# One decoder layer on one core: ten operand splits handed from VectorE to GpSimd, and the attention masks written earlier in a visit

## The chip, the core and the metric

The kernel runs on one core of a Trainium2 chip. Five engines work beside each other: TensorE (PE in the profile, its weight loads PEld), VectorE (DVE), ScalarE (ACT), GpSimd (POOL) and SyncE (SP), which here only issues transfers. Each engine works through its own list of instructions in order; what stands on which list, and where, is settled when the program is built. The metric is the device time of one execution in microseconds (us), the median over several runs.

## The reference

One layer: a normalised input times one wide matrix gives the inputs of a state-space branch and of an attention branch. Both end in a projection, are gated and added, and go through `w_out`, a second norm and the residual. What matters here is the attention with its forgetting term, and the projection of the state-space branch.

```
for blk in range(seqlen // 128):
    q0, q1 = blk * 128, (blk + 1) * 128
    s = einsum('bhqd,bhkd->bhqk', q[:, :, q0:q1], k[:, :, :q1]) * scale
    s = s + fcum[:, :, q0:q1, None] - fcum[:, :, None, :q1]
    s = where(kpos <= qpos, s, -inf)
    outs.append(einsum('bhqk,bhkd->bhqd', softmax(s), v[:, :, :q1]))
...
p_ssm = einsum('ble,ed->bld', y_ssm, w_branch_ssm)
p_att = einsum('ble,ed->bld', y_att, w_branch_att)
merged = sigmoid(g_ssm) * p_ssm + sigmoid(g_att) * p_att
```

The sequence has 1024 positions, the model 1024 columns, and there are 16 heads of 64.

## The kernel before, in words

**Products.** Every wide product is done for a pair of 128 output columns with seven block products in place of eight (`Pair`, `Stream`), so the 1024 x 1024 moving matrix is turned into seven operands: `b11`, `b21`, `-b22` and the differences `t1`, `-t2`, `t3`, `t4`. In this order they lie in the tiles x0 to x6. Each operand has four slabs of 128 x 512 (index j), so one matrix makes 28 blocks. Each block is kept as a high part in a reduced format (x0h and so on) and a low part, the remainder (x0l): three matmuls with high and low parts replace one. `Operands.split` (line 265) makes them: ScalarE copies the raw block into the high part (line 278, or 275 with a sign), and VectorE subtracts it from the raw block, which leaves the low part (line 279, or 276). Column weights are split in the same way (lines 350 and 351, `wop`).

**Replacing operands.** There is one set of operand tiles. When the last product that reads an operand of one matrix is done, its tile is loaded with the next matrix's block and split. `ops_s` (line 1166) holds the operands of the state-space branch's output, which replace those of the layer's input late in the attention. `ops_a` and `ops_w` follow later.

**Attention.** Eight pairs of heads are worked through in six visits each (the loop at line 1697, m = 0 to 47; hp is the pair, g the visit in it). A visit computes scores for two query blocks against one half of the keys (`scores`, line 1491): TensorE writes `s`, VectorE adds the forgetting rows `fb` and finds the minimum (line 1512; a block in which a mask is needed reads a masked copy in the free end of `ex` in place of `fb`), ScalarE takes the exponential (line 1516). TensorE turns the result (`turned`, tile pt), ScalarE and, for one block in four, VectorE copy it to `p` (lines 1555 and 1553), and the next visit multiplies it with the values (`weighted`, tile av). Turning and scores share four PSUM buffers, so scores of a visit need the copies of the visit before. Between these steps the visit places half products of the stream (`stream.halves`), which fill TensorE's time.

**Masks.** `mask` (line 1374) adds a triangle to 128 columns of `fb` in place, `masked` (line 1383) writes a masked copy into `ex`; both are pairs of GpSimd instructions. In the kernel before they are called at the end of `loads(m)` (line 1625), behind the visit's first half products and their chores.

**Order.** Instructions given to `pin` keep the order in which the program is written; the others are placed by the scheduler that builds the lists. All masks, splits and most stores on GpSimd's list are pinned, so whatever waits there holds up all that stands behind it. Without a pin are the four stores of the gates `ga` that go out by GpSimd (`tanh_gate`, line 645).

Of the kernel before, what the change touches and what calls it, by code (L numbers as in the profile page):

```python
# [12 lines left out]
ALU = mybir.AluOpType  # L13
# [6 lines left out]
NK = D // P  # L20
# [66 lines left out]
def hybrid_layer(ctx: ExitStack, tc, a, out):  # L87

    nc = tc.nc
# [31 lines left out]
    ys_dram = tc.dram_tile([NK, P, T], F32, name="ys_dram")  # L121
# [11 lines left out]
    def pin(op):  # L133
        return tc.keep_in_program_order(op)
# [24 lines left out]
    class Operands:  # L159
# [6 lines left out]
        BLOCKS = {"b11": (0, 0), "b12": (0, 1), "b21": (1, 0), "b22": (1, 1)}  # L166
        LESS = {"t1": ("b12", "b11"), "t2": ("b22", "t1"), "t3": ("t2", "b11"), "t4": ("t2", "b21")}

        def __init__(self, name, src, there=lambda k, h: True, order=lambda op: op, queue=nc.gpsimd):
            self.src, self.there, self.order, self.queue = src, there, order, queue  # L170
            self.copy = src
            self.tiles, self.left, self.made, self.at, self.step = {}, {}, set(), {}, 0
            self.lows, self.most, self.lag = {}, 1, {}
            self.dram = {n: tc.dram_tile([KH, P, HALF], F32, name=f"{n}_{name}") for n in self.LESS}
# [90 lines left out]
        def split(self, name, j, raw=None):  # L265
            h, l = (t[:, j, :] for t in self.tiles[name])
            if name.strip("-") in self.lows:

                pin(nc.scalar.activation(h, h.bitcast(F32), AF.Copy, scale=-1.0 if name[0] == "-" else 1.0))
                self.left[name].remove(j)  # L270
                return
            if raw is None:
                raw = l.bitcast(F32)
            if name[0] == "-":
                pin(nc.scalar.activation(h, raw, AF.Copy, scale=-1.0))
                pin(nc.vector.scalar_tensor_tensor(l, raw, -1.0, h, ALU.mult, ALU.subtract))
            else:
                pin(nc.scalar.activation(h, raw, AF.Copy))
                pin(nc.vector.tensor_tensor(l, raw, h, ALU.subtract))
            self.left[name].remove(j)  # L280

        def direct(self, j, y, x):
# [192 lines left out]
    class Stream:  # L475
# [74 lines left out]
        def half(self):  # L550
            if self.run is None:
                if self.at == len(self.steps):
                    return False
                p, which = self.steps[self.at]
                if which == 7 and p.ops is ops_a and "merged" not in fin:
                    return False
                if p.ops is ops_a and not all(p.ops.ready(OPERAND[which].strip("-"), j) for j in range(KH)):
                    return False
                self.ahead(False)
                for ops in self.building:  # L560
                    ops.some(OPERAND[which])
                if self.at + 1 < len(self.steps):
                    after, then = self.steps[self.at + 1]
                    after.begin(then, after.sums + (after is p and which in (5, 7)), True)
                self.run = p.do(which)
                next(self.run)
            else:
                for _ in self.run:
                    pass
                self.run = None  # L570
                p, which = self.steps[self.at]
                if p in self.following:
                    ops = self.following[p]
                    if ops not in self.building:
                        self.building.append(ops)
                    ops.open(OPERAND[which])
                self.ahead(True)
                self.at += 1
            for ops in self.building:
                if self.held is None:  # L580
                    ops.some()
                else:
                    self.held.append(ops)
            for chores in (self.chores, self.line):
                if chores:
                    chore = chores.pop(0)
                    if chore:
                        chore()
            self.count += 1
            for w in self.waiting:  # L590
                w[0] -= 1
            for w in [w for w in self.waiting if w[0] <= 0]:
                self.waiting.remove(w)
                w[1]()
            return True
# [39 lines left out]
    def tanh_gate(dram, i, queue=nc.scalar):  # L635

        t = {}

        def dst(ch):
            t[ch] = small()  # L640
            return t[ch]

        def post(ch):
            nc.scalar.activation(t[ch], t[ch], AF.Tanh, scale=0.5)
            queue.dma_start(dram[i, :, half(ch)], t[ch])

        return dst, post

# [514 lines left out]
        return dst, post, begin  # L1163

    attended = set()
    ops_s = Operands("s", lambda k, h: ys_dram[k, :, half(h)])
    ops_a = Operands("a", lambda k, h: ya_dram[k, :, half(h)], lambda k, h: (k, h) in attended)
    ops_w = Operands("w", lambda k, h: a["wo"][k * P : (k + 1) * P, half(h)], order=pin, queue=nc.sync)
    ops_a.most = 2
# [167 lines left out]
    with tc.tile_pool(name="att", bufs=1, reuse_waits="tile", side="right") as ap, tc.tile_pool(  # L1337
# [36 lines left out]
        def mask(hp, i):  # L1374

            f = fb[hp, i // 4][:, :, i % 4 * P : i % 4 * P + P]
            for e in range(2):
                pin(nc.gpsimd.tensor_tensor(f[:, e], f[:, e], far[:, P:], ALU.add))
# [246 lines left out]
        def loads(m):  # L1625

            hp, g = divmod(m, 6)
            more = hp + 1 < NK
            if g == 0:
                if hp:  # L1630
                    load_v(hp, 0)
                if not m:

                    for j in range(KH):
                        stream.line += ops_s.differences(j, difference_tile, small)
            if g == 1:
                load_q(hp, (3, 0))
            if g == 2 and more:
                load_k(hp + 1, 1)
            if g == 3:  # L1640
                load_q(hp, (2, 1))
                if more:
                    load_v(hp + 1, 1)
                if hp >= KH:
                    state["t"] = difference_tile()
                    nc.sync.dma_start(state["t"], ops_a.block("t1", hp - KH))
            if g == 4 and more:
                load_q(hp + 1, (7, 4))
            if g == (5 if more else 4) and hp >= KH:
                state["y"] = fetched("b11", hp - KH)  # L1650
            if g in (1, 3, 4):
                mask(hp, {1: 6, 3: 3, 4: 2}[g])
            if g == 4 and more:
                mask(hp + 1, 7)
            if g == 4:
                masked(hp, 1)
            if g == 5 and more:
                masked(hp + 1, 4)
            if g == 5 and more:
                load_k(hp + 1, 0)  # L1660
                load_q(hp + 1, (6, 5))

        def end(m):

# [32 lines left out]
        for m in range(6 * NK + 1):  # L1697

            if m < 6 * NK:
                hp, g = divmod(m, 6)  # L1700
                if not g:
                    heads[hp] = Heads(hp)
                for u in range(2):
                    scores(hp, g, u)
            for one in made:
                weighted(*one)
            for hd, which in end(m - 1):
                hd.free(which)
            if m == 6 * NK:
                stream.release()  # L1710
                heads[NK - 1].out(2)
                break
            for hd, which in end(m - 2):
                if hd.last and which and m < 6 * NK - 1:
                    hd.out(which)
            for fn in deferred:
                fn()
            deferred.clear()
            stream.release()
            for hd, which in end(m):  # L1720
                hd.settle(which)
            ahead, behind = room(m)
            stream.halves(ahead)

            for hd, which in end(m):
                hd.scale(which)
                hd.load_gates(which)
            if m == 6 * NK - 1:
                heads[hp].out(1)
                for fn in deferred:  # L1730
                    fn()
                deferred.clear()
            loads(m)
            made = turned(hp, g, list(end(m - 1)))
            if g in (1, 3):
                masked(hp, {1: 5, 3: 0}[g])
            for hd, which in end(m - 2):
                if not hd.last or not which:
                    hd.out(which)
            if m == 6 * NK - 1:  # L1740
                tp = pp.tile([P, HALF], F32, tag="s", bufs=4, name="tp")
                heads[hp].turn(2, tp)
                heads[hp].send(2, tp)
            stream.hold()
            stream.halves(behind)
            for hd, which in end(m if m == 6 * NK - 1 else m - 1):
                hd.take(which)
# [59 lines left out]
```

## Time and profile before

| | |
|---|---|
| three runs | 1264.94, 1266.55, 1267.89 us; median 1266.55 |
| profiled execution | 1264.74 us, its span 1263.0 us, granted TensorE clock 0.999 |
| busy share of the span | PE 98%, PEld 78%, DVE 81%, ACT 63%, POOL 27% |
| attention | from about 656 to 1105 us; the blocks of `ops_s` are split between 904 and 967 us |

Times in the views are counted in us from the start of the span. A row of the timeline gives start, length, engine, line and operation, the tiles (out<-in), shape and count, and in brackets the idle time ahead of it with the instruction that ended it. DVE instructions that follow each other overlap a little: one of 128 x 512 takes 0.69 us and the next starts 0.60 us after it. PE counts as busy until the modelled end of a matmul, so a short wait is partly hidden in the row ahead of it; the length of a run of like matmuls shows it.

### The profile page before, as it was taken

How to read it: one execution, taken by the hardware profiler on the slowest of the kernel's cores; microseconds unless marked ns; L12 is line 12 of the kernel's file. 1: busy time of each engine (PE TensorE's matmuls, PEld its weight loads, DVE VectorE, ACT ScalarE, POOL GpSimd, SP SyncE). 2: the span in 40 equal slices, each digit the busy share in tenths (PEclk: the TensorE clock that was granted, in tenths of full speed). 3: DMA queues.
4: the chain of work that ended last, by engine and by line, in shares of the span. 5: the costliest groups of instructions: out<-in, count | busy, mean ns of one | idle time of the engine just before them, and what ended most of it. 6: DMA issues, size and time to landing. Idle time of an engine off the chain costs nothing.

```text
span 1263.0 us, 20876 instructions
## 1 busy us (share of the span) xinstructions
PE 1234.3 (98%) x6864; PEld 985.6 (78%) x6864; DVE 1018.9 (81%) x1989; ACT 789.7 (63%) x1735; POOL 337.0 (27%) x384
## 2 busy tenths in 40 slices
PE   5999999999999999999999999999999999999997
PEld 3688888888888888888887777777776777688886
DVE  7998886888789878998666677776899778797975
ACT  7745765556655765567555666666786666743753
POOL 4000440014300241015111333433122232357062
PEclk9999999999999999999999999999999999999999
DMA  8243442645446542854465576666787557756932
GB/s 298 70 125 85 146 151 98 199 150 184 129 128 203 171 140 91 241 154 131 133 210 193 182 250 207 215 203 211 259 301 255 197 195 252 254 196 206 366 118 99
DMA packets 162476, 233.57 MB, mean 185 GB/s; under 512 B 15200, under 2 KB 73024, under 8 KB 162368
## 3 DMA queue, kind: packets, MB, share of 16 engines
q1 hardware_dynamic: 140160, 196.08, 48.6%
q10 hardware_dynamic: 16704, 18.06, 4.0%
q0 software_dynamic: 5504, 18.09, 3.7%
q8 instruction: 54, 0.88, 0.3%
q14 instruction: 54, 0.44, 0.1%
HBM read 162.99 MB, written 72.34 MB: 186 GB/s over the span
## 4 chain that ended last, share of the span: by engine, by line
PE 80%; DMA 7%; DVE 7%; ACT 3%; issue 2%; SPq 1%; POOL 0%; DVEq 0%; ACTq 0%; POOLq 0%
PE pb L128 34%; PE pc L128 20%; PE pd L128 7%; PE av L128 5%; PE pt L131 4%; PE s L128 4%; PE yps L128 2%; DVE wop L351 1%; PE st L128 1%; DMA xt<-in_x 1%; DVE ex L1512 1%; DMA raw<-in_wu 1%; PE tr L131 1%; PE tr_v L131 1%; DVE sum L356 1%
## 5 line engine op out<-in xcount | busy, mean ns | idle before, releaser
L350 ACT ACTIVATE wop<-sum 128x512 fp32r<-128x512 f32 x180 | 112.2, 626 | 106.3 <-DVE sum L356 49.6
L351 DVE TENSOR_TENSOR wop<-sum,wop 128x512 fp32r<-128x512 f32 x180 | 138.7, 772 | 47.6 <-ACT wop L350 45.8
L1516 ACT ACTIVATE ex<-ex,nm 128x512 f32<-128x512 f32 (+1 forms) x192 | 116.3, 607 | 75.6 <-DVE nm L1512 74.1
L410 ACT ACTIVATE s<-pb 128x512 f32<-128x512 f32 x143 | 84.6, 592 | 93.5 <-PE pb L128 91.4
L128 PE MATMUL pb<-x0h,wop 128*128 128x512 f32 x384 | 132.3, 400 | 0.0
L128 PE MATMUL pc<-x2h,wop 128*128 128x512 f32 x384 | 130.2, 397 | 0.0
L128 PE MATMUL pc<-x3h,wop 128*128 128x512 f32 x384 | 129.8, 396 | 0.4 <-DVE ot L427 0.4
L128 PE MATMUL pb<-x4h,wop 128*128 128x512 f32 x384 | 129.1, 395 | 0.0
L128 PE MATMUL pb<-x6h,wop 128*128 128x512 f32 x376 | 126.7, 395 | 1.3 <-ACT s L410 1.3
L128 PE MATMUL pb<-x5h,wop 128*128 128x512 f32 x376 | 126.8, 395 | 0.2 <-ACT s L410 0.2
L351 DVE TENSOR_TENSOR wop<-raw,wop 128x512 fp32r<-128x512 f32 x144 | 107.6, 748 | 18.5 <-ACT wop L350 18.5
L350 ACT ACTIVATE wop<-raw 128x512 fp32r<-128x512 f32 x144 | 89.7, 624 | 19.8 <-PE pd L128 10.5
L1512 DVE CUSTOM_DVE_ANT_0 ex<-s,fb 128x512 f32<-128x512 f32 (+1 forms) x128 | 78.6, 653 | 22.6 <-PE s L128 22.5
L128 PE MATMUL pd<-x1h,wop 128*128 128x512 f32 x288 | 95.8, 392 | 0.0
L211 POOL TENSOR_TENSOR wd<-wd 128x256 f32<-128x256 f32 x32 | 32.3, 1011 | 203.1 <-DMA wd<-in_wo 124.3
L128 PEld LDWEIGHTS pc<-x3h,wop 128*128 128x128 f32 x384 | 72.1, 188 | 17.7 <-issue 2.4
L128 PEld LDWEIGHTS pc<-x2h,wop 128*128 128x128 f32 x384 | 72.1, 188 | 17.5 <-issue 2.0
L128 PEld LDWEIGHTS pb<-x4h,wop 128*128 128x128 f32 x384 | 72.1, 188 | 17.2 <-issue 2.5
L128 PEld LDWEIGHTS pb<-x0h,wop 128*128 128x128 f32 x384 | 72.7, 189 | 16.1 <-issue 1.5
L128 PEld LDWEIGHTS pb<-x6h,wop 128*128 128x128 f32 x376 | 70.6, 188 | 17.7 <-ACT s L410 1.7
L128 PEld LDWEIGHTS pb<-x5h,wop 128*128 128x128 f32 x376 | 70.6, 188 | 16.7 <-issue 1.5
L131 PE MATMUL pt<-ident,ex 128*128 128x128 f32 x576 | 76.2, 274 | 2.7 <-ACT ex L1516 1.2
(311 smaller groups left out, 3025.5 us busy)
## 6 DMA issues: line engine op xcount, KB each, us to landing
raw<-in_wu SPq DMA_DIRECT2D x128, 256.0 KB
csb<-cs_dram SPq DMA_DIRECT2D x32, 256.0 KB
q<-q_dram SPq DMA_DIRECT2D x32, 256.0 KB
k<-k_dram SPq DMA_DIRECT2D x16, 512.0 KB
fb<-f_dram SPq DMA_DIRECT2D x16, 512.0 KB
rb<-st_dram SPq DMA_DIRECT2D x48, 128.0 KB
wd<-in_wo SPq DMA_DIRECT2D x40, 128.0 KB
xt<-in_x SPq DMA_DIRECT2D x8, 512.0 KB
```

Source lines behind the costliest of these rows:

```text
L128: return tc.keep_in_program_order(nc.tensor.matmul(*args, **kw))
L131: return tc.keep_in_program_order(nc.tensor.transpose(out_, in_, idn))
L211: pin(nc.gpsimd.tensor_tensor(t[out_], t[a_], t[b_], ALU.subtract))
L350: nc.scalar.activation(op[:, 0], src, AF.Copy)
L351: nc.vector.tensor_tensor(op[:, 1], src, op[:, 0], ALU.subtract)
L356: self.adds.tensor_tensor(t, x, y, ALU.add)
L410: nc.scalar.activation(s, ps, AF.Copy)
L1512: nc.vector.tensor_tensor_reduce(o, s[e][:, 0:w], f[:, e], 1.0, 3.0e38, ALU.add, ALU.min, nm)
L1516: pin(nc.scalar.activation(o, o, AF.Exp, scale=-1.0, bias=nm, accum_out=hd.at(hd.sm, i, h, e)))
```

## The change

Three edits. `Operands` gets an engine `less`, and `ops_s` is made with GpSimd: of the five operands without a sign (x0, x1, x3, x5, x6) the blocks with odd j, ten of 28, have their low part subtracted by GpSimd. The masks move from `loads` into a function of their own, called right behind the visit's scores and `settle`, ahead of its first half products; at g = 4 the copy for the next visit now comes ahead of the mask for the next pair. The four `ga` stores on GpSimd's list are pinned.

```
-        def __init__(self, name, src, there=lambda k, h: True, order=lambda op: op, queue=nc.gpsimd):
+        def __init__(self, name, src, there=lambda k, h: True, order=lambda op: op, queue=nc.gpsimd, less=nc.vector):
...
                 pin(nc.scalar.activation(h, raw, AF.Copy))
-                pin(nc.vector.tensor_tensor(l, raw, h, ALU.subtract))
+                pin((self.less if j % 2 else nc.vector).tensor_tensor(l, raw, h, ALU.subtract))
...
-            queue.dma_start(dram[i, :, half(ch)], t[ch])
+            order = pin if queue is nc.gpsimd else lambda op: op
+            order(queue.dma_start(dram[i, :, half(ch)], t[ch]))
...
-    ops_s = Operands("s", lambda k, h: ys_dram[k, :, half(h)])
+    ops_s = Operands("s", lambda k, h: ys_dram[k, :, half(h)], less=nc.gpsimd)
...
-            if g in (1, 3, 4):
-                mask(hp, {1: 6, 3: 3, 4: 2}[g])
-            if g == 4 and more:
-                mask(hp + 1, 7)
-            if g == 4:
-                masked(hp, 1)
-            if g == 5 and more:
-                masked(hp + 1, 4)
...
+        def masks(m):
+            hp, g = divmod(m, 6)
+            more = hp + 1 < NK
+            if g in (1, 3, 4):
+                mask(hp, {1: 6, 3: 3, 4: 2}[g])
+            if g == 4:
+                masked(hp, 1)
+                if more:
+                    mask(hp + 1, 7)
+            if g == 5 and more:
+                masked(hp + 1, 4)
...
                 hd.settle(which)
+            masks(m)
             ahead, behind = room(m)
             stream.halves(ahead)
```

TensorE's list stays as it is. On GpSimd's list, before, this stands at the visits g = 4 and 5 of the fifth pair of heads (about 919 to 943 us in the trace). A row with fb is `mask`, one with ex is `masked`.

```order
L1378 TENSOR_TENSOR fb<-fb,far 128x128 x2
L1387 TENSOR_TENSOR ex<-fb,far 128x128 x2
L645 DMA ga_dram<-th 128x512
L1378 TENSOR_TENSOR fb<-fb,far 128x128 x4
L1387 TENSOR_TENSOR ex<-fb,far 128x256 x2
L645 DMA ga_dram<-th 128x512
L1387 TENSOR_TENSOR ex<-fb,far 128x128 x2
```

The same place now (lines 1378, 1387 and 645 have become 1379, 1388 and 646).

```order
L1388 TENSOR_TENSOR ex<-fb,far 128x128 x2
L279 TENSOR_TENSOR x1l<-x1l,x1h 128x512
L1379 TENSOR_TENSOR fb<-fb,far 128x128 x2
L1388 TENSOR_TENSOR ex<-fb,far 128x256 x2
L1379 TENSOR_TENSOR fb<-fb,far 128x128 x2
L646 DMA ga_dram<-th 128x512
L279 TENSOR_TENSOR x1l<-x1l,x1h 128x512
L279 TENSOR_TENSOR x5l<-x5l,x5h 128x512
L1388 TENSOR_TENSOR ex<-fb,far 128x128 x2
L279 TENSOR_TENSOR x5l<-x5l,x5h 128x512
```

The copy of 256 columns was behind a store and four mask instructions; it is now behind one subtraction and two. Three subtractions stand ahead of the next copy of 128 columns, or between it and the stores.

On VectorE's list, before, the second visit of these (g = 5, about 933 to 939 us) reads as follows. Line 1512 is the scores' pass; 128x384 is the first query block, 128x256 the masked one.

```order
L1512 ISA ex,nm<-s,fb 128x384
L1512 ISA nm 128x1
L351 TENSOR_TENSOR wop<-raw,wop 128x512
L279 TENSOR_TENSOR x5l<-x5l,x5h 128x512 x2
L1512 ISA ex,nm<-s,ex 128x256
L1512 ISA nm 128x1
L1512 ISA ex,nm<-s,ex 128x256
L1512 ISA nm 128x1
L1427 RECIPROCAL sm<-sm 128x8
```

The same place now (1512 has become 1513, 1427 has become 1428).

```order
L1513 ISA ex,nm<-s,fb 128x384
L1513 ISA nm 128x1
L1513 ISA ex,nm<-s,ex 128x256
L1513 ISA nm 128x1
L351 TENSOR_TENSOR wop<-raw,wop 128x512
L1513 ISA ex,nm<-s,ex 128x256
L1513 ISA nm 128x1
L279 TENSOR_TENSOR x5l<-x5l,x5h 128x512
L1428 RECIPROCAL sm<-sm 128x8
```

The first masked pass now follows the unmasked ones at once, the second stands behind one weight split, and the x5 subtraction stands behind both.

Two visits later (about 948 to 956 us) VectorE's list before has five subtractions between the copy of a turned block and the end of the visit's four passes (the fifth, of x6, stands behind the last pass).

```order
L1553 COPY p<-pt 128x2x128
L279 TENSOR_TENSOR x3l<-x3l,x3h 128x512
L356 TENSOR_TENSOR sum<-raw 128x512
L279 TENSOR_TENSOR x3l<-x3l,x3h 128x512
L279 TENSOR_TENSOR x6l<-x6l,x6h 128x512
L1512 ISA ex,nm<-s,fb 128x512
L1512 ISA nm 128x1
L351 TENSOR_TENSOR wop<-raw,wop 128x512
L279 TENSOR_TENSOR x6l<-x6l,x6h 128x512
L1512 ISA ex,nm<-s,fb 128x512
```

Now (1553 has become 1554) there is one, and none ahead of the first pass.

```order
L1554 COPY p<-pt 128x2x128
L356 TENSOR_TENSOR sum<-raw 128x512
L1513 ISA ex,nm<-s,fb 128x512
L1513 ISA nm 128x1
L351 TENSOR_TENSOR wop<-raw,wop 128x512
L279 TENSOR_TENSOR x6l<-x6l,x6h 128x512
L1513 ISA ex,nm<-s,fb 128x512
```

Of the other four, one x3 subtraction stands earlier in VectorE's list, and the x3 and the two x6 ones with odd j are GpSimd's. SyncE's list differs in five single transfers that change places with a neighbour, ScalarE's in some ten rows at the visit around 941 us. Near the end of the attention (about 1101 us) one x3 subtraction of `ops_a` now stands behind the second masked pass in place of ahead of it.

More of the change, by code (lines that the diff above doesn't have):

```diff
@@ L167, in hybrid_layer @@
         LESS = {"t1": ("b12", "b11"), "t2": ("b22", "t1"), "t3": ("t2", "b11"), "t4": ("t2", "b21")}
-        def __init__(self, name, src, there=lambda k, h: True, order=lambda op: op, queue=nc.gpsimd):
-            self.src, self.there, self.order, self.queue = src, there, order, queue
+        def __init__(self, name, src, there=lambda k, h: True, order=lambda op: op, queue=nc.gpsimd, less=nc.vector):
+            self.src, self.there, self.order, self.queue, self.less = src, there, order, queue, less
             self.copy = src
```

## The prediction

> **What bounds the kernel now.** I read the page's busy times first, then the busy time by stretches, then what TensorE waited for, then the timeline of the stretch that stood out, engine by engine. The page:
>
> ```profile
> PE 1234.3 (98%) x6864; PEld 985.6 (78%) x6864; DVE 1018.9 (81%) x1989; ACT 789.7 (63%) x1735; POOL 337.0 (27%) x384
> ```
>
> TensorE is the bound over the span, so an edit that leaves its list alone can gain only what TensorE waits. Busy time by stretch (columns: length, then busy time and instructions of PE, PEld, DVE, ACT, POOL, then clock, DMA share, GB/s), around the place where the blocks are split:
>
> ```profile
> 904.00:930.00 26.00, 26.00 (x172) 19.89 (x169) 22.84 (x60) 20.73 (x53) 3.33 (x6) 1.00 0.88 297
> 930.00:976.00 46.00, 43.57 (x285) 32.25 (x284) 43.58 (x106) 35.16 (x91) 13.94 (x25) 1.00 0.80 267
> 976.00:1050.00 74.00, 74.00 (x502) 57.06 (x501) 56.69 (x150) 46.26 (x124) 19.98 (x40) 1.00 0.62 207
> ```
>
> Ahead of 930 and behind 976 TensorE has no idle time; between them 46.00 - 43.57 = 2.43 us, and there VectorE is as busy as TensorE. What TensorE waited for in that stretch (total, times, longest):
>
> ```profile
> PE s L128 <- DVE p L1553: 1.1, 2, 0.7
> PE pt L131 <- DVE nm L1512: 0.6, 2, 0.4
> PE s L128 <- ACT p L1555: 0.3, 1, 0.3
> PE pt L131 <- ACT ex L1516: 0.2, 1, 0.2
> ```
>
> VectorE's copies and score passes come late; the exponential that ended one wait follows such a pass. The lengths show what the modelled ends hide. PE's rows, the first two not held up:
>
> ```profile
> 917.46 1.91 PE L131 MATMUL pt<-ident,ex 128*128 128x128 f32 x16
> 927.95 1.03 PE L131 MATMUL pt<-ident,ex 128*128 128x128 f32 x8
> ...
> 936.41 0.38 PE L131 MATMUL pt<-ident,ex 128*128 128x128 f32 x2
> 937.17 0.96 PE L131 MATMUL pt<-ident,ex 128*128 128x128 f32 x5 [0.39 <-DVE nm L1512]
> 938.30 0.55 PE L131 MATMUL pt<-ident,ex 128*128 128x128 f32 x3 [0.16 <-ACT ex L1516]
> ...
> 949.07 1.66 PE L128 MATMUL s<-k,q 64*128 64x512 f32 x12 [0.65 <-DVE p L1553]
> ...
> 954.80 2.31 PE L131 MATMUL pt<-ident,ex 128*128 128x128 f32 x16
> ...
> 959.76 0.61 PE L128 MATMUL s<-k,q 64*128 64x256 f32 x5 [0.44 <-DVE p L1553]
> ...
> 973.41 0.49 PE L131 MATMUL pt<-ident,ex 128*128 128x128 f32 x3
> 974.15 1.99 PE L131 MATMUL pt<-ident,ex 128*128 128x128 f32 x13 [0.25 <-DVE nm L1512]
> ```
>
> Sixteen turns take 1.91 us, eight 1.03, so one is 0.11 and ten are 1.25. From 936.41 ten took 938.85 - 936.41 = 2.44: 1.2 lost. At 949.07 0.65. From 954.80 sixteen took 2.31: 0.4 lost. At 959.76 0.44. From 973.41 sixteen took 976.14 - 973.41 = 2.73: 0.8 lost. Together 3.5 us behind VectorE, and 0.3 behind ScalarE's copies.
>
> **The change part by part.** VectorE's rows at these places:
>
> ```profile
> 934.11 0.98 DVE L351 TENSOR_TENSOR wop<-raw,wop 128x512 fp32r<-128x512 f32 x1
> 935.02 1.76 DVE L279 TENSOR_TENSOR x5l<-x5l,x5h 128x512 fp32r<-128x512 f32 x2
> 936.70 0.41 DVE L1512 CUSTOM_DVE_ANT_0 ex<-s,ex 128x256 f32<-128x256 f32 x1
> ...
> 940.61 0.68 DVE L279 TENSOR_TENSOR x5l<-x5l,x5h 128x512 fp32r<-128x512 f32 x1
> ...
> 948.59 0.42 DVE L1553 COPY p<-pt 128x256 f32<-128x256 f32 x1
> ...
> 959.02 0.68 DVE L1553 COPY p<-pt 128x512 f32<-128x512 f32 x1
> ```
>
> *The subtractions.* Ten of VectorE's go, each 0.68 us long and 0.60 of its list: 10 x 0.60 = 6.0 us. GpSimd gets ten. It has none on such an operand now; the nearest rows are its differences of the same shape, 1.28 us, and they show what VectorE pays for them. First pair: a subtraction while VectorE starts a weight split, whose two inputs lie in SBUF. Second pair: a subtraction while VectorE makes a score pass, one input of which lies in PSUM.
>
> ```profile
> 823.33 1.28 POOL L211 TENSOR_TENSOR x<-x,th 128x512 f32<-128x512 f32 x1 [0.88 <-DMA th<-ys_dram]
> ...
> 791.40 1.29 POOL L211 TENSOR_TENSOR x<-x,th 128x512 f32<-128x512 f32 x1 [7.69 <-DMA x<-ys_dram]
> ```
>
> ```profile
> 823.38 1.77 DVE L351 TENSOR_TENSOR wop<-raw,wop 128x512 fp32r<-128x512 f32 x1 [2.03 <-ACT wop L350]
> ...
> 791.42 0.69 DVE L1512 CUSTOM_DVE_ANT_0 ex<-s,fb 128x512 f32<-128x512 f32 x1
> ```
>
> The split took 1.77 in place of 0.69: held for 1.08, nearly all of GpSimd's 1.28. The pass was not held. So a subtraction on GpSimd costs VectorE between 0 and 1.08 us, against the 0.60 that it saves; net -0.60 to +0.48 each. I take half, 0.55, since VectorE's list there goes to and fro between the two kinds: the ten then give it next to nothing in the sum (10 x (0.55 - 0.60) = -0.5 us), and what counts is where each falls.
>
> [...]
>
> *The masks.* Ahead of the masked passes GpSimd and ScalarE did this:
>
> ```profile
> 931.40 2.51 POOL L1378 TENSOR_TENSOR fb<-fb,far 128x128 f32<-128x128 f32 x4
> 933.87 1.75 POOL L1387 TENSOR_TENSOR ex<-fb,far 128x256 f32<-128x256 f32 x2
> ```
>
> ```profile
> 928.86 1.14 ACT L278 ACTIVATE x1h<-x1l 128x512 fp32r<-128x512 f32 x2
> ...
> 942.87 0.72 ACT L1516 ACTIVATE ex<-ex,nm 128x512 f32<-128x512 f32 x1 [0.28 <-DVE nm L1512]
> ...
> 948.57 1.10 ACT L1555 ACTIVATE p<-pt 128x256 f32<-128x256 f32 x3
> ...
> 961.51 0.61 ACT L1516 ACTIVATE ex<-ex,nm 128x384 f32<-128x384 f32 x1 [3.37 <-DVE nm L1512]
> ```
>
> The masked copy was there at 933.87 + 1.75 = 935.62. Now one subtraction (x1, j = 1) and two mask instructions stand ahead. That subtraction waits for ScalarE's first pair of x1 copies, which precedes the row of 928.86, so it ends about 928.9 + 1.28 = 930.2; two masks (half of 2.51) and the copies (1.75) end at 933.2, before the unmasked passes end at 934.1. So the first masked pass starts about 934.1 in place of 936.70, and the second after one split, about 935.1 in place of 937.1 (936.70 + 0.41): two microseconds earlier, more than the 1.2 that TensorE lost from 936.41. Gain 1.2 there.
>
> Part of that is given back at 949.07. TensorE would come 1.2 earlier to scores that wait for copies of turned blocks, VectorE's at 948.59 and ScalarE's from 948.57. Both hang on VectorE's passes just ahead of 942.87, where ScalarE takes up the exponential behind them and works on to its copies. Ahead of those passes VectorE loses one x5 subtraction (940.61) and gets one x3 subtraction, comes up to 1.0 earlier, and can be held by one of GpSimd's x5 subtractions: 1.0 - 0.55 = 0.45 earlier at the copies, between 1.0 and -0.5 (two holds). So of what is won at 937, 0.45 is kept at 949.
>
> *Between 949 and 960* VectorE loses four subtractions, 2.4 us, and GpSimd's x3 and x6 fall here, two or three holds of 0 to 1.08: 0 to 2.4 earlier. TensorE lost 0.4 and 0.44; I take 0.7 of 0.84.
>
> *From 973.41* 0.8 was lost because the passes of that visit ran late; ScalarE's pause of 3.37 ahead of 961.51 shows that the backlog is there with the passes of the visit before. If the copy at 959.02 comes half a microsecond earlier, so do they, and their followers: 0.7 of 0.8.
>
> *At the end* one x3 subtraction of `ops_a` goes behind the second masked pass. VectorE's two rows, then ScalarE's and TensorE's:
>
> ```profile
> 1100.67 0.68 DVE L279 TENSOR_TENSOR x3l<-x3l,x3h 128x512 fp32r<-128x512 f32 x1
> 1101.28 0.41 DVE L1512 CUSTOM_DVE_ANT_0 ex<-s,ex 128x256 f32<-128x256 f32 x1
> ```
>
> ```profile
> 1101.73 0.51 ACT L1516 ACTIVATE ex<-ex,nm 128x256 f32<-128x256 f32 x1 [0.35 <-DVE nm L1512]
> ```
>
> ```profile
> 1102.38 0.55 PE L131 MATMUL pt<-ident,ex 128*128 128x128 f32 x3 [0.62 <-ACT ex L1516]
> ```
>
> The pass comes 0.60 earlier, ScalarE's exponential by its pause of 0.35, TensorE with it: 0.35.
>
> *At nothing* I cost the rest. The two x0 subtractions between 905 and 911 fall where TensorE has no idle time; if both hold VectorE, the passes there come a microsecond later, which the work in hand hides. The stores that now stand behind masks or subtractions on GpSimd's list (`ga`, `ya`, the differences) are read much later; the masks of the other visits come earlier where nobody waited. The moved transfers on SyncE's list change places with one neighbour. The pinned `ga` stores wait for ScalarE's gate and could hold up the masks behind them; in the visit shown the copy of 256 columns is ahead of the store.
>
> Sum: 0.45 + 0.7 + 0.7 + 0.35 = 2.2 us. The profiled execution took 1264.74 us (span 1263.0, 1.74 around it) and would take 1262.5. It lies 1.8 below the median of the three runs, 1266.55, from which I forecast: 1266.55 - 2.2 = 1264.35, so 1264.4. A measurement of this kernel tells some 0.2% (2.5 us) from no change, so this forecast is "same", on the faster side.
>
> **The rivals.** *All of it is gained.* If GpSimd's subtractions fall beside score passes and copies, as at 791.40, VectorE is rid of 6.0 us where it is the last to arrive, and all 3.5 us go, with 0.35 at the end: 1266.55 - 3.85 = 1262.7. For it: much of VectorE's list in the stretch reads PSUM, as its costliest group there (count, busy us, mean ns), 6.5 us, against 3.0 for the costlier group of those weight splits that stay and have two SBUF inputs:
>
> ```profile
> L1512 DVE CUSTOM_DVE_ANT_0 ex<-s,fb 128x512 f32<-128x512 f32 x10 | 6.5, 690 | 0.0
> L351 DVE TENSOR_TENSOR wop<-raw,wop 128x512 fp32r<-128x512 f32 x4 | 3.0, 760 | 0.0
> ```
>
>  Against it: a subtraction becomes ready when ScalarE's copy ends, which is when VectorE's own subtraction of the same operand becomes ready too.
>
> *ScalarE is as late.* Its copies from 948.57 start with VectorE's, and it has lost no work. Then the early masks are given back at 949, the later waits stay ScalarE's, and about 0.4 remains: 1266.15. The order also allows that the masks gain little, since the copy of 256 columns has a subtraction ahead of it.
>
> *Slower, by holds.* Each subtraction meets an instruction with two SBUF inputs: +0.48 each on VectorE. Eight (all but x0's) lie where VectorE was busy 43.58 of 46.00: 8 x 0.48 = 3.8 us on the path of TensorE's copies, less 1.2 from the masks: 1266.55 + 2.6 = 1269.2. It decides once the mean hold is above 0.9 us. Against it: the pass rows, which aren't held.
>
> **How the numbers follow.** Forecast 0.42 (1262.9 to 1266.2 by the bounds of its terms), full gain 0.28, ScalarE as late 0.17, holds 0.13. Faster by over 0.2% (under 1264.0): the full gain and 0.12 of the forecast's, 0.40. Slower: 0.11 of the holds. Same: 0.49. The range reaches from 1262.0, below the full gain, to 1267.2, above the third case by what the three runs differ; it leaves out most of the holds and the tails, under 0.2.
>
> **What would show it.** Right: ten GpSimd rows of line 279 of about 1.3 us between 904 and 956; the first masked pass straight behind the unmasked ones near 934; turns at 936 unbroken; TensorE's idle time in the stretch of 46 us down from 2.4 to about 1. VectorE's weight splits beside GpSimd's subtractions near 1.7 would show the holds, and their sum over the ten, 5 to 6 us, that the relief is used up. Wrong: TensorE's wait for the copy at 949 grown beyond 1.5 us, a masked pass that waits for GpSimd, or a new wait behind 976.

## The result and the profile after

| | median, us | runs | before beside it | ratio, 95% interval |
|---|---|---|---|---|
| changed kernel | 1268.32 | 22 | 1265.67 (22 runs) | 1.0023 [1.0016, 1.0030] |

The change makes the kernel slower, by 2.7 us between the medians and 2.9 by the ratio. The page of the profile after, and its stretches (columns as before):

```profile
PE 1235.6 (98%) x6864; PEld 986.9 (78%) x6864; DVE 1019.1 (80%) x1979; ACT 788.9 (62%) x1735; POOL 353.8 (28%) x394
```

```profile
904.00:930.00 26.00, 26.00 (x174) 19.98 (x175) 22.05 (x56) 20.72 (x52) 6.59 (x9) 1.00 0.87 292
930.00:976.00 46.00, 41.58 (x269) 30.86 (x268) 44.30 (x92) 33.09 (x85) 24.24 (x30) 1.00 0.76 256
976.00:1050.00 74.00, 73.87 (x495) 57.09 (x495) 55.65 (x150) 47.53 (x127) 21.71 (x40) 1.00 0.61 201
1107.44:1110.85 3.41, 3.41 (x9) 2.48 (x8) 3.25 (x6) 2.04 (x6) 0.54 (x1) 0.50 0.28 109
```

VectorE has ten instructions fewer and is busy for as long as before (1019.1 us, 1018.9 before): what it was relieved of came back as longer instructions. TensorE's idle time between 930 and 976 went from 2.43 to 46.00 - 41.58 = 4.42 us, 1.99 more. The last row, at half clock, is a second loss, taken up in the last section. What TensorE waited for between 926 and 976, and its rows at the places of the prediction:

```profile
PE s L128 <- DVE p L1554: 4.0, 3, 2.3
```

```profile
932.32 1.15 PE L128 MATMUL s<-k,q 64*128 64x384 f32 x12 [1.01 <-DVE p L1554]
...
937.49 1.25 PE L131 MATMUL pt<-ident,ex 128*128 128x128 f32 x10
...
950.85 1.67 PE L128 MATMUL s<-k,q 64*128 64x512 f32 x12 [2.26 <-DVE p L1554]
...
962.13 0.62 PE L128 MATMUL s<-k,q 64*128 64x256 f32 x5 [0.75 <-DVE p L1554]
```

The ten turns at 937 are unbroken, as forecast. The list holds waits for one thing only, VectorE's copies of turned blocks, and they have grown. Long rows of VectorE there, then GpSimd's:

```profile
929.32 1.78 DVE L279 TENSOR_TENSOR x1l<-x1l,x1h 128x512 fp32r<-128x512 f32 x1
...
936.12 1.53 DVE L279 TENSOR_TENSOR x5l<-x5l,x5h 128x512 fp32r<-128x512 f32 x1
...
941.04 0.91 DVE L279 TENSOR_TENSOR x3l<-x3l,x3h 128x512 fp32r<-128x512 f32 x1
941.87 1.49 DVE L1486 TENSOR_TENSOR zr<-o 128x256 f32<-128x256 f32 x1
...
947.44 1.82 DVE L279 TENSOR_TENSOR x3l<-x3l,x3h 128x512 fp32r<-128x512 f32 x1
...
950.39 0.41 DVE L1554 COPY p<-pt 128x256 f32<-128x256 f32 x1
...
953.30 1.97 DVE L351 TENSOR_TENSOR wop<-raw,wop 128x512 fp32r<-128x512 f32 x1
...
962.00 2.22 DVE L1478 TENSOR_TENSOR zr<-o,rb 128x512 f32<-128x512 f32 x1
```

```profile
929.12 1.43 POOL L279 TENSOR_TENSOR x1l<-x1l,x1h 128x512 fp32r<-128x512 f32 x1 [8.19 <-DMA x5l<-t_s]
...
941.36 1.72 POOL L279 TENSOR_TENSOR x5l<-x5l,x5h 128x512 fp32r<-128x512 f32 x1
...
947.43 1.28 POOL L279 TENSOR_TENSOR x3l<-x3l,x3h 128x512 fp32r<-128x512 f32 x1 [2.03 <-ACT x3h L278]
```

VectorE's even block and GpSimd's odd block of an operand start together, as ScalarE's copies of the two stand next to each other: 929.32 beside 929.12, 947.44 beside 947.43. VectorE's takes 1.78 and 1.82 us in place of 0.69. The second of these stands three instructions ahead of the copy at 950.39 for which TensorE waited 2.26 us. The copy itself, from PSUM, takes its usual 0.41. The weight split of 1.97 us, 0.68 elsewhere, stands beside GpSimd's subtraction of x6 at 953.43.

TensorE's list is the same in all kernels here, so the same matmul can be laid beside itself: its start after minus its start before is its shift. For the matmuls that before starts at 925, 934, 940, 948, 953, 962 and 978 us the shift is +0.61, +1.12, -0.10, +0.17, +1.77, +2.38 and +2.59 us. So TensorE loses 0.5 us at 931, gains 1.2 from 936 to 940, loses 1.6 at 949 and goes on losing in smaller steps. What the shift grows by from 920 to 978 I call the **loss in the stretch**; here it is +1.99.

### The profile page after: what moved, and what is told of

The parts are those of the page before. It is cut to its first block, busy times and chain, and to the rows that moved or that the text cites. A ratio compares the mean times of both kernels' runs of the same rounds, so it can differ in the third digit from the quotient of the medians.

```text
span 1267.0 us, 20882 instructions
## 1 busy us (share of the span) xinstructions
PE 1235.6 (98%) x6864; PEld 986.9 (78%) x6864; DVE 1019.1 (80%) x1979; ACT 788.9 (62%) x1735; POOL 353.8 (28%) x394
## 4 chain that ended last, share of the span: by engine, by line
PE 80%; DMA 8%; DVE 6%; ACT 4%; issue 2%; SPq 0%; POOL 0%; DVEq 0%; ACTq 0%; POOLq 0%
PE pb L128 34%; PE pc L128 20%; PE pd L128 6%; PE av L128 5%; PE pt L131 4%; PE s L128 4%; PE yps L128 2%; DVE wop L351 1%; PE st L128 1%; DMA xt<-in_x 1%; DMA raw<-in_wu 1%; DMA xr<-in_x 1%; PE tr L131 1%; PE tr_v L131 1%; DVE ex L1513 1%
## 5 line engine op out<-in xcount | busy, mean ns | idle before, releaser
L128 PE MATMUL pc<-x3l,wop 128*128 128x512 f32 x192 | 75.8, 395 | 1.3 <-DVE x3l L279 1.3
```

The costliest lines, as they stand in the source:

```text
L128: return tc.keep_in_program_order(nc.tensor.matmul(*args, **kw))
```

## The experiments

"Idle" is TensorE's idle time in the 46 us of 930 to 976 (before: 2.43). Times are medians of 6 to 12 runs, ratios are to runs of before on the same chip; the last two columns are from the one profiled execution of each kernel.

| run | time / before, us | ratio, 95% interval | idle | loss in the stretch |
|---|---|---|---|---|
| e1 masks alone | 1266.95 / 1266.67 | 1.0011 [0.9997, 1.0025] | 3.56 | +2.84 |
| e15 the same again | 1268.31 / 1268.13 | 1.0002 [0.9989, 1.0015] | 1.66 | -0.39 |
| e2 subtractions alone | 1272.18 / 1266.67 | 1.0047 [1.0035, 1.0060] | 6.30 | +8.57 |
| e3 one input | 1265.19 / 1266.67 | 0.9991 [0.9982, 1.0000] | 1.92 | -1.63 |
| e4 twenty | 1277.07 / 1266.67 | 1.0089 [1.0073, 1.0104] | 10.76 | +9.85 |
| e5 masks, y by GpSimd | 1265.14 / 1266.87 | 0.9984 [0.9972, 0.9997] | 0.41 | -1.71 |
| e12 the same again | 1266.24 / 1266.30 | 1.0000 [0.9989, 1.0012] | 1.67 | -0.36 |
| e13 masks, y early | 1267.49 / 1268.13 | 0.9998 [0.9986, 1.0010] | 0.57 | -1.73 |
| e11 x0 alone, y by GpSimd | 1264.61 / 1266.30 | 0.9987 [0.9976, 0.9998] | 0.91 | -1.39 |
| e6 quarters | 1273.47 / 1266.87 | 1.0050 [1.0034, 1.0066] | 6.81 | +7.39 |
| e7 extra, two inputs | 1271.69 / 1266.87 | 1.0033 [1.0022, 1.0044] | 4.61 | +6.03 |
| e8 extra, one input | 1268.68 / 1266.87 | 1.0010 [0.9999, 1.0022] | 3.20 | +1.74 |
| e9 changed kernel, y by GpSimd | 1268.58 / 1266.30 | 1.0019 [1.0010, 1.0028] | 3.47 | +2.04 |
| e10 before, y by GpSimd | 1270.59 / 1266.30 | 1.0037 [1.0024, 1.0050] | 1.77 | +0.59 |
| e14 breaks | 1271.22 / 1268.13 | 1.0028 [1.0016, 1.0040] | 5.14 | +3.70 |

### The two halves of the change, the second input, and twice the dose

e1 takes `less=nc.gpsimd` away from `ops_s`, so all subtractions are VectorE's again. e2 is the kernel before with `less` alone. e4 gives GpSimd all twenty subtractions of the five operands (`self.less` in place of `self.less if j % 2 else nc.vector`). e3 replaces GpSimd's ten and leaves the low parts of these blocks at zero:

```
-                pin((self.less if j % 2 else nc.vector).tensor_tensor(l, raw, h, ALU.subtract))
+                if j % 2 and self.less is nc.gpsimd:
+                    pin(nc.gpsimd.tensor_single_scalar(l, h.bitcast(F32), 0.0, ALU.mult))
+                else:
+                    pin(nc.vector.tensor_tensor(l, raw, h, ALU.subtract))
```

> The moved masks and the ordered gate stores alone; all 28 subtractions stay with VectorE. Theory of the holds (GpSimd's ten subtractions keep VectorE out just where its copies are the last to arrive, and cost more than they hand back): without them the gain of the masks at 937 us (1.2 to 1.4 us) and at 1102 us (0.4 us) is left, less what the next wait takes back: 0.8 to 2.0 us faster than before, some 1264.3 us where before takes 1265.7. Rival of the masks (their new place, or the order that comes with it, is what costs the 2.65 us): 1 to 3 us slower than before, 1267 to 1269 us.

> GpSimd's ten subtractions alone; the masks and the gate stores stay as before. Theory of the holds: all of the loss and the gain of the masks on top of it, 3 to 5 us slower than before, some 1269.5 us. Rival of the masks: within 0.7 us of before.

> As the changed kernel, but at the place of each of the ten subtractions GpSimd multiplies the high part by zero: one input from SBUF in place of two, as many elements written. The low parts of ten of 28 blocks are left out of the computation by it. Theory of the holds, if the hold belongs to instructions with two inputs: VectorE keeps the ten subtractions' 6 us and loses nothing, 1.5 to 3 us faster than before, some 1263.3 us, and the copies behind a GpSimd instruction take their shortest time again. If an instruction with one input holds VectorE as well: as the changed kernel, 1268.3 us. Rival of the latency (a block's low part is ready later because GpSimd takes twice VectorE's time and queues it behind masks): as the changed kernel too, but with the copies at their shortest.

> As the changed kernel, but GpSimd subtracts all twenty low parts of these five operands, not ten. Theory of the holds: about twice the cost of the ten (2.65 us and the 1 to 2 us that the masks gain, so 4 us for ten): 5 to 7.5 us slower than before, some 1271.8 us. Rival of the masks: as the changed kernel, 1268.3 us, within 0.7 us.

The masks alone don't cost what the change costs, but gain nothing either: the expectation of 0.8 to 2.0 us was a miss. The subtractions alone cost 5.5 us by the medians, more than the whole change and more than the 3 to 5 expected, and twenty cost 10.4, above the 5 to 7.5 expected. With one input in place of two, at the same places, the loss is gone and the time lies 1.5 us under before, at the edge of its interval. So the subtractions lose the time, and what they read matters. (In e3 the low parts are zero as well; the pair e7 and e8 below is free of that.)

How they lose it is told by the rows of e2: VectorE's instruction just behind a copy, then what GpSimd did.

```profile
930.18 4.69 DVE L372 TENSOR_TENSOR sum<-sum,raw 128x512 f32<-128x512 f32 x1
```

```profile
930.23 1.31 POOL L279 TENSOR_TENSOR x1l<-x1l,x1h 128x512 fp32r<-128x512 f32 x1
931.48 1.58 POOL L1378 TENSOR_TENSOR fb<-fb,far 128x128 f32<-128x128 f32 x4
933.02 1.30 POOL L1387 TENSOR_TENSOR ex<-fb,far 128x256 f32<-128x256 f32 x2
```

An addition of 0.68 us took 4.69: not one GpSimd instruction long, but the whole run of them, to 934.3. In e4 the same happened to an instruction of 128 x 8 elements that takes 0.17 us elsewhere; its row, the first and last of GpSimd's there, and TensorE's:

```profile
936.27 10.84 DVE L1429 TENSOR_SCALAR ns<-sm 128x8 f32<-128x8 f32 x1
```

```profile
935.84 2.54 POOL L279 TENSOR_TENSOR x1l<-x1l,x1h 128x512 fp32r<-128x512 f32 x2
...
944.01 0.56 POOL L646 DMA_DIRECT2D ga_dram<-th  x1
944.59 2.49 POOL L279 TENSOR_TENSOR x3l<-x3l,x3h 128x512 fp32r<-128x512 f32 x2
```

```profile
947.76 2.18 PE L128 MATMUL s<-k,q 64*128 64x512 f32 x11 [7.48 <-DVE p L1554]
```

It ended at 947.11, when GpSimd's list paused (944.59 + 2.49 = 947.08), and the copy of p behind it let TensorE stand 7.48 us.

The 1.78 and 1.82 us in the changed kernel are 0.69 and nearly one GpSimd subtraction (1.43 and 1.28 us beside them). 4.69 and 10.84 us are longer than any one GpSimd instruction beside them: a subtraction takes 1.31 us in e2, and two take 2.47 to 2.54 in e4.

### Does a hold end with the instruction?

e6 writes each of GpSimd's ten subtractions as four of 128 columns. e14 puts a memset of a small tile ahead of and behind each:

```
+                    for c in range(0, HALF, P):
+                        cs = slice(c, c + P)
+                        pin(nc.gpsimd.tensor_tensor(l[:, cs], raw[:, cs], h[:, cs], ALU.subtract))
```

```
+                    pin(nc.gpsimd.memset(tick, 0.0))
                     pin(nc.gpsimd.tensor_tensor(l, raw, h, ALU.subtract))
+                    pin(nc.gpsimd.memset(tick, 0.0))
```

> As the changed kernel, but each of GpSimd's ten subtractions is written as four of 128 columns. Theory of the chain (VectorE gets no turn between GpSimd's two-input instructions that follow one another without a pause, so that the hold is as long as the chain: 10.84 us on one 0.17 us instruction in the run with twenty): the cut gives VectorE nothing, and four starts in place of one make the chains longer, 1268 to 1272 us. Rival (a hold ends with the instruction): at most 0.4 us is left of each hold, and the time falls by 1 to 2.5 us under the changed kernel, some 1266.5 us.

> The changed kernel with a memset of 128x8 on GpSimd, without an input, ahead of and behind each of its ten subtractions. Theory of the chain: VectorE gets a turn wherever the chain of two-input instructions is broken, so no VectorE instruction takes over 2 us, and the time falls under the changed kernel by 0.5 to 2 us, some 1267 us. Rival (the hold lasts while GpSimd is busy with anything): single VectorE instructions of 3 us and more, and 1268 to 1273 us.

Quarters are slower than the changed kernel, by 0.27% or 3.4 us as the ratios to before have it, and above the 1272 us that the theory of the chain allowed. The small instruction on `sm` is held again, for 7.46 us (VectorE, then TensorE):

```profile
934.65 7.46 DVE L1434 TENSOR_SCALAR ns<-sm 128x8 f32<-128x8 f32 x1
```

```profile
943.29 1.22 PE L128 MATMUL s<-k,q 64*128 64x512 f32 x4 [5.35 <-DVE p L1559]
```

So cutting a subtraction doesn't let VectorE in. The breaks gain nothing either. The theory of the chain wanted no VectorE instruction over 2 us and a shorter time; the longest is 2.10, where the changed kernel has 2.22, and the time is no better. Neither forecast came true in full. VectorE's longest in the stretch:

```profile
951.32 2.10 DVE L286 TENSOR_TENSOR x6l<-x6l,x6h 128x512 fp32r<-128x512 f32 x1
```

What decides is left open. In the changed kernel GpSimd also works from 937.96 to 944.92 without a pause, and VectorE gets through, at 0.88 to 1.49 us an instruction, with GpSimd's own subtractions stretched to 1.72 and 1.77, from 1.28. In e2, e4 and e6 an instruction of VectorE waits for a whole run. So does line 1478 at 962.00 in the changed kernel, for a store and two moved masks: 2.22 us, and 2.22 in e1, where GpSimd makes no subtraction of line 279, against 0.77 before. So the moved masks can hold VectorE too; the prediction had their new places at nothing. That a hold can be as long as the run is shown; when it is, is not.

### The price of a hold by itself

Here the masks are moved and VectorE keeps all subtractions. Behind ten of them GpSimd works on the finished low part in place, with two inputs (e7) or one (e8), without changing it:

```
+                    lv = l.rearrange("p (a b) -> p a b", b=64)
+                    pin(nc.gpsimd.tensor_tensor(lv, lv, zeros.unsqueeze(1).to_broadcast([P, 8, 64]), ALU.subtract))
...
+                    pin(nc.gpsimd.tensor_single_scalar(lv, lv, 1.0, ALU.mult))
```

> Masks moved, all 28 subtractions with VectorE, and behind ten of them GpSimd subtracts a tile of zeros from the low part, in place: an instruction of two inputs that takes no work off VectorE. Theory of the holds: their price without what is handed back, 3 to 8 us slower than before, 1269.5 to 1274.5 us; single VectorE instructions of over 1.5 us in the trace. Rival (the latency of a low part that GpSimd has to finish is what costs): the same time as the next run, with one input.

> As the run before, but GpSimd's extra instruction multiplies the low part by one, in place: one input from SBUF, at the same places and with the same dependences. Theory of the holds: within 2 us of the masks alone (1267 to 1269 us), and 2 us or more under the run with two inputs. Rival of the latency: the same time as with two inputs, within 1 us.

The pair differs by 3.0 us in the medians, and by 4.29 in the stretch, at the same places and with the same dependences. The second input makes it, with the operation that takes it. The stretch of 930 to 976, e7 then e8:

```profile
930.00:976.00 46.00, 41.39 (x244) 29.90 (x244) 44.00 (x89) 32.46 (x81) 25.02 (x29) 0.93 0.75 237
```

```profile
930.00:976.00 46.00, 42.80 (x270) 31.69 (x269) 43.83 (x98) 34.53 (x86) 26.22 (x30) 0.96 0.76 263
```

The latency of a low part that GpSimd has to finish is in both, and GpSimd's instructions with one input are even the longer ones, 1.48 to 1.86 us against 1.27 to 1.66 (e3, with one input, has 1.49 to 1.93, where the changed kernel, with two, has 1.28 to 1.77). VectorE tells them apart: between 926 and 960 none of its instructions takes over 1.10 us in e8, and the longest takes 1.78 in e7. What that latency and a hold by one input cost together is too small to be seen: e8 stands at 1.0010, the masks alone at 1.0011 and 1.0002.

### Where the masks' gain went

In e1 the gain came (-1.2 us from 936 to 940) and was lost at 949. VectorE's rows, then TensorE's:

```profile
942.99 0.68 DVE L427 TENSOR_TENSOR th<-s,pc 128x512 f32<-128x512 f32 x1
946.54 0.69 DVE L1603 TENSOR_TENSOR y<-x,y 128x512 f32<-128x512 f32 x1 [2.87 <-DMA x6l<-t_s]
...
949.42 0.41 DVE L1554 COPY p<-pt 128x256 f32<-128x256 f32 x1
```

```profile
949.89 1.85 PE L128 MATMUL s<-k,q 64*128 64x512 f32 x12 [3.47 <-DVE p L1554]
951.67 2.40 PE L128 MATMUL av<-p,v 128*64 128x256 f32 x16
```

VectorE came to line 1603 early and stood 2.87 us for a load: its input y, issued by SyncE at 937.16 behind loads of k, fb, q, raw and x6l. (The view names the x6l load beside it; the last piece of y landed at 946.32, and VectorE went on within 0.03 us.) e5 issues y by GpSimd; e13 keeps SyncE and loads y a visit earlier (`if g == 4 and hp >= KH`), ahead of rb, k and fb. e9 and e10 give the changed kernel and the one before GpSimd's issue, and e11 leaves only x0's two subtractions with GpSimd:

```
-                state["y"] = fetched("b11", hp - KH)
+                state["y"] = fetched("b11", hp - KH, nc.gpsimd)
```

> As the moved masks alone, but the load of y (L1577) is issued by GpSimd, on its own queue, and no longer stands on SP's queue behind 2 to 3 MB of other loads. In the run of the masks alone VectorE stood 2.87 us before L1603 for a load, its copy of p came at 949.42 us, and TensorE waited 3.47 us at 949.89 us and ran the next 3.41 us at half clock. Theory of the load (the masks' gain of 2 us at 938 us is given back because y lands at 946.5 us, whatever is earlier): the wait before L1603 falls under 0.5 us, TensorE's wait at 949 us to at most 1 us, and the time is 1.5 to 3 us under before, some 1264.3 us where before takes 1266.5. Rival (another load, or VectorE's own work, is as late as y): within 1 us of the masks alone, which took 0.3 us more than before.

> The changed kernel with the load of y issued by GpSimd. VectorE did not stand for y in the changed kernel, so by the theory of the holds nothing of the ten subtractions' cost goes: 2.5 to 4.5 us over the masks with the same load, which took 1265.1 us, so 1267.6 to 1269.6 us. Rival (the loss of the changed kernel came through the loads): within 1 us of the masks with that load.

> The kernel before with the load of y issued by GpSimd, and nothing else. VectorE did not stand for y there either, as its copy of p was late by itself: within 0.8 us of before if the load is only a second limit, 1.5 us or more faster if the load is what the masks with that load gained by.

> The masks with the load of y issued by GpSimd, and of the ten subtractions only the two of x0 on GpSimd, at 905 to 911 us, where no wait of TensorE was seen within 20 us. Theory of the holds, with the place deciding: two holds of 0.27 us cost nothing there, within 0.8 us of the masks with that load, 1265.1 us. Rival (every subtraction on GpSimd costs its share of what ten cost, 3 to 5 us): 0.6 to 1 us slower than the masks with that load.

> The masks with the load of y issued by GpSimd once more, beside the three others: 1.5 to 3 us faster than before by the theory of the load as the second limit.

> The moved masks alone, with y loaded one visit earlier, on SP's queue, ahead of the loads of rb, k and fb behind which it stood. Theory of the load as the second limit: VectorE doesn't stand before L1603, TensorE waits at most 1 us at 949 us, and the time is 1 to 3 us under the masks alone beside it. Rival (ScalarE's copy of p or VectorE's own work is as late): within 0.7 us of the masks alone.

> The moved masks alone once more, beside the two others: within 1 us of before, as VectorE stands for y, and TensorE waits 3 us or more at 949 us.

The stretch, in e13 and then in e15, where y landed at 945.45 and VectorE stood 0.48 us for it:

```profile
930.00:976.00 46.00, 45.43 (x293) 34.12 (x292) 44.59 (x110) 36.32 (x95) 10.49 (x20) 1.00 0.83 279
```

```profile
930.00:976.00 46.00, 44.34 (x286) 32.72 (x285) 44.12 (x107) 35.22 (x92) 10.06 (x19) 1.00 0.83 275
```

With y out of the way TensorE's idle time falls to 0.41 and 0.57 us (e5, e13), and 1.7 us of the stretch are gained. The prediction had 1.85 there for the whole change, 0.45 by the masks and 1.4 by VectorE's relief; here the masks do it with VectorE's subtractions all in place. In e12, the same kernel as e5, VectorE did not stand for y either, but TensorE waited 1.2 us at 951 for ScalarE's copy of p, and 0.36 us are left of the gain: ScalarE is the third in the row, as one of the rivals had it. With y as it was, the two profiles say +2.84 and -0.39: it depends on when the load lands. In the times this is too small to be shown: 0.9984, 1.0000 and 0.9998 with y moved against 1.0011 and 1.0002 without. They point the right way, and no single comparison settles it. Three expectations were missed: e12 was to gain 1.5 to 3 us on before, e13 1 to 3 us on e15 (it gained 0.8), and in e15 TensorE was to wait 3 us or more at 949 (it waited 0.60).

e9 stands 2.3 us above e12, which ran beside it, and its long rows are those of the changed kernel (1.77, 1.53, 1.49, 1.83 and 1.97 us), so the subtractions' loss does not come through that load. x0's two subtractions cost nothing at 910 to 913, where TensorE has work in hand (e11, the only one of these beside e5 whose interval lies under 1). They hardly met VectorE either: its one lengthened row beside them took 0.88 us. So e11 doesn't tell the place from the collision. e10 missed its 0.8 us by far and says little as a control: its profile loses 2.5 us at 1061, where TensorE waited 2.36 us for an exponential, behind ScalarE's wait of 2.9 us for a store of y; the stretch shows +0.59.

## Why the prediction was wrong

2.2 us less were forecast, 2.7 to 2.9 more were measured.

**The masks at 937: right.** 1.2 us forecast, 1.2 measured, and the turns are unbroken. It was closer than the forecast had it: the masked copies ended at 934.49 in place of 933.2, as GpSimd's instructions were stretched, and the first masked pass started at 934.83.

**The subtractions' sum: about right.** "The ten then give it next to nothing in the sum": VectorE's busy time moved by 0.2 us. What VectorE's rows beside GpSimd's ten take over the shortest of their kind adds up to some 7 us, 0.7 each in place of 0.55.

**Where each falls: wrong, and this decided.** The step that failed is "1.0 - 0.55 = 0.45 earlier at the copies", and with it the 0.7 "between 949 and 960". VectorE's copy came at 950.39 in place of 948.59, so 1.8 us later, or 1.2 without the 0.61 by which TensorE lay behind at 925. In place of one hold of 0.55, five of VectorE's instructions between 939.39 and 949.2 were lengthened by 2.9 us together, those of 1.49 and 1.82 the most. A relief that is even in the sum isn't even in place. The odd block on GpSimd starts with the even one on VectorE, so a hold falls on the instructions just ahead of a copy that TensorE waits for, as at 947.44. From 941 to 949 TensorE gave back 1.9 us in place of 0.75. It lost 0.6 between 955 and 960 in place of a gain of 0.7, and 0.5 at 931 where nothing was forecast. From 968 to 976 it lost 0.2 in place of gaining 0.7. The bounds failed too: 0 to 1.08 us for a hold came from one pair of rows, with a single GpSimd instruction. Where GpSimd had a run of them, 4.69, 7.46 and 10.84 us were seen.

**The end: the gain came and was given back.** 0.35 was forecast as kept. TensorE's turns at 1102 gained 0.45, and a product two microseconds behind them lost 0.43 again. TensorE before and after, then VectorE before and after:

```profile
1104.30 0.50 PE L128 MATMUL pc<-x3l,wop 128*128 128x512 f32 x1 [0.89 <-DVE x3l L279]
```

```profile
1106.80 0.50 PE L128 MATMUL pc<-x3l,wop 128*128 128x512 f32 x1 [1.32 <-DVE x3l L279]
```

```profile
1102.95 0.69 DVE L1483 TENSOR_TENSOR o<-o,rb 128x512 f32<-128x512 f32 x1 [0.17 <-DMA rb<-st_dram]
```

```profile
1105.44 0.69 DVE L1484 TENSOR_TENSOR o<-o,rb 128x512 f32<-128x512 f32 x1 [0.60 <-DMA rb<-st_dram]
```

VectorE stood longer for the load of rb, and the x3 subtraction that TensorE waits for stands right behind that instruction. In every kernel here with the moved masks TensorE waits 1.3 to 1.9 us at this place (and in e10, whose order differs there as well), in e2 0.9 as before.

**The rivals.** The slower one, by holds, is what happened (1269.2 forecast, 1268.3 measured), though the mean hold stayed under the 0.9 us from which it was to decide. So its number is partly luck: not the mean decided but the place. ScalarE was not as late: in the changed kernel it stood idle ahead of its exponential until VectorE's pass came:

```profile
944.00 0.73 ACT L1517 ACTIVATE ex<-ex,nm 128x512 f32<-128x512 f32 x1 [2.81 <-DVE nm L1513]
```

**What the sum left out.** First, the loads of y and rb, second limits close behind the first. The profile of before shows no wait of VectorE for y and 0.17 us for rb, as VectorE itself came late. Second, the clock. The mean granted clock of the changed kernel's 22 timed runs is 0.9971, that of before in the four sets beside the experiments 0.9979 to 0.9983; 0.001 of 1263 us is 1.3 us, an estimate. With the loss in the stretch, and nothing left of the gain at the end, that makes 2.0 + 1.3 = 3.3 us, somewhat over the measured 2.7 to 2.9. The first term is from one profiled execution, so this fits no better than roughly.

## What to carry to other kernels

Moving ten elementwise instructions with two inputs from VectorE to GpSimd was no relief here: VectorE's busy time went from 1018.9 to 1019.1 us, as its instructions beside them took up to 1.97 us in place of 0.68. Count the hold, and count it where it falls: ahead of which copy or pass. Look for a moved instruction that becomes ready together with one that stays: here the two collided (929.32 beside 929.12, 947.44 beside 947.43, and VectorE's took 1.78 and 1.82 us in place of 0.69). Before an early step is given a gain, look for what the next instruction behind it reads, and when that lands: the gain at 937 went to the load of y in e1, and the gain at 1102 to the load of rb.

## What the runs showed of the hardware

**VectorE can be kept out for a whole run of GpSimd instructions**, a DMA issue among them in e4: up to 10.84 us for an instruction of 0.17. VectorE's instructions that read PSUM were not seen lengthened: no copy of p and no score pass took over 0.69 us, in the changed kernel between 904 and 976, in e2, e4, e6 and e7 between 932 and 944.

**TensorE's clock drops by half for 3.41 us after a wait, or doesn't.** The trace has the granted clock. In e1, behind the wait of 3.47 us:

```profile
951.18:954.59 3.41, 3.41 (x21) 2.12 (x18) 3.41 (x8) 1.52 (x4) 0.00 (x0) 0.50 0.60 206
```

Sixteen products with the values took 2.40 us there in place of 1.31. In the changed kernel's trace the clock is full until 1107.44 us, halved for 3.413 and full again for 153.60, 45 times as long; the stretch ahead, from 22.00, is 318 times as long, and before's one full stretch, 21.04 to 1260.08, 363 times. So in these two traces the stretches are whole numbers of steps of 3.41 us, whose bounds lie differently in each. The mean clock from 930 to 976 fits this in the others: 0.96 in e1, e8 and e9, 0.93 in e6, e7 and e14, 0.89 in e2 and e4, where one, two or three halved steps in 46 us make 0.963, 0.926 and 0.889; in the other nine it is 1.00. So a wait can cost 1.7 us more (half of 3.41) in one execution and nothing in another: the longest wait there was 2.3 us in both e9 and the changed kernel, with 0.96 and 1.00. That it goes by where the wait falls in the steps is my reading of such pairs, and not shown. In the changed kernel the wait of 2.26 us at 949 was split between two steps (from 947.02 and 950.43, TensorE busy for 0.46 and 0.88 of them by the modelled ends) and halved nothing, and the step with the wait of 1.32 us ahead of 1106.80, busy for 0.57, was followed by half clock from 1107.44 on (the last row of the stretches above). Another step, from 175.60, was busy for 0.55 and none was halved behind it, so what decides is not shown. From 1100 to 1150 the mean clock is 0.97 in the changed kernel, e3 and e4, where TensorE waited 1.3, 1.9 and 1.7 us at that place, and 1.00 in e1, with 1.4, and in before and e2, with 0.9. These are too few to say that the longer wait is what lowered the mean clock of the timed runs. Before's profiled execution had full clock from 21 to 1260 us, and lay 0.9 us under the median of 22 runs.
